# A decoder layer with 32 experts on one core: half of w_down taken with the expert groups, and half of the gate summed over eight chunks in PSUM

## The chip, the cores and the metric

The kernel runs on one core of a Trainium2 chip. The metric is the device time of one execution in microseconds (us); a profiled execution shows in addition its span, from the first to the last instruction of the trace. All positions ("at 372.0 us") are counted from the span's start.

## The reference, cut to what matters

One layer on 256 tokens of width 2048, all in fp32: attention, then a mixture of 32 experts (top 2 of one group of 8), then a gate, then a norm.

```
m   = rms_norm(h)
hid = silu(m @ w_gate[e]) * (m @ w_up[e]) * combine[:, e]     # 32 experts, 2048 -> 256
h   = h + sum over e of hid[e] @ w_down[e]                    # 256 -> 2048
n   = rms_norm(h)
h   = h + sigmoid(n @ w_ple_gate) * (p @ w_ple)              # 2048 -> 2048, 256 -> 2048
out = rms_norm(h)
```

The weights of this part have to be read once: w_gate and w_up 64 MiB each, w_down 64 MiB, w_ple_gate 16 MiB, w_ple 2 MiB.

## The kernel before

**Groups of experts.** The experts are taken four at a time, in 8 groups g = 0 to 7. Each expert holds at most 32 tokens, so a group's rows fill the 128 partitions. `gather` (in group 0 `first_rows` with its `part` and `turn`, one 512-column block each) picks the tokens with 0/1 matmuls and writes them, transposed, to `xg`. `hidden` multiplies them by the weights: 16 loads of 1 MiB per group, taken in quarters (k, i) of four loads, k for w_gate or w_up and i for the first or second half of the 2048 rows. The result, transposed, stays in `hid_all` to the end. Then `load_down`, `places` (the place mask `pw`, which holds the token's weight where the token stands), `down` (the product `dn`, copied to `y`) and `spread_rows` (y put back to its tokens, in plain fp32, and added to `acc[0]`) do block 0 of w_down, which is columns 0 to 511.

**The tail.** The other 1536 columns of w_down come after the last group, in `BLOCKS` 1 to 4 (512, 512, 256 and 256 columns), because the gate's input n needs a block of h that is complete. A pass over a block has units `u`: one group each in blocks 1 and 2 (8 units), two groups each in blocks 3 and 4 (4 units). A unit loads 2 MiB of w_down (`load_rows`), makes the product (`down_rows`, which splits the weighted result into a high part `y_hi` and a low part `y_lo` in the fast format fp32r) and adds it to the tokens' rows (`add_rows`, with 0/1 masks `held`, made by `weigh` during block 1). Between the two it takes some pieces of the gate of the block that was finished before (`PACE` says how many). One piece is 128 rows by 512 columns of w_ple_gate, cut into `wh` on ScalarE and `wl` on VectorE (`split_w`, two pieces ahead) and used in six matmuls (L974 to L976). `operand` transposes a finished block into `n_hi` and `n_lo`. Each block's gate is summed in PSUM over its own 4 (or 2) chunks of 128 rows and then copied or added to `z` by ScalarE or VectorE (L1040, L1042). The last unit of block 4, the last two chunks of the gate and the final norm follow (`last_rows_in`, `last_operand`, `finish`, `norm_rows`).

**The ring.** All weights go through 22 slots of 1 MiB (`Ring`). A load takes the slot that was used longest ago and waits until its last reader is done; `keep=True` holds a slot for good. SP issues all these loads in the order in which the code asks for them. `acc[1]` to `acc[3]` take two slots before group 7, `extra` and `emb` take three before group 2, `n_hi`, `n_lo` and `y` take five at the tail's start.

**The branch.** Before group 7 a branch (L901, `tc.If`) leads to `overflow`, for experts with more than 32 tokens; it isn't taken on these inputs. Every engine passes it; SP has half of group 7's 16 loads of w_gate and w_up ahead of it and half behind it.

Of the kernel before, what the change touches and what calls it, by code (L numbers as in the profile page):

```python
# [44 lines left out]
ON_V = (0, 1, 2, 3, 4)  # L45
CUT_G = (0, 5, 6)
# [39 lines left out]
def layer(ctx, tc, T, out):  # L86
# [628 lines left out]
    def load_experts(g, k):  # L715


        ws = []
        name, v = (("wg", w_gate), ("wu", w_up))[k]
        for i in range(2):  # L720
            parts = []
            for q in range(4):
                e = 4 * g + q
                if (g, k, i, q) == (0, 1, 1, 3):
                    w = hid_all.rearrange("p g c r -> p (g c r)").rearrange("p (c f) -> p c f", f=DE)
                else:
                    w = ring.tile([P, NC // 2, DE], name)
                if g:
                    nc.sync.dma_start(w, v[e].rearrange("(p c) f -> p c f", c=NC)[:, 8 * i : 8 * i + 8, :])
                else:  # L730
                    nc.sync.dma_start(
                        w.rearrange("p (b c) f -> p b c f", b=2),
                        v[e].rearrange("(b p c) f -> p b c f", b=4, c=4)[:, 2 * i : 2 * i + 2],
                    )
                parts.append(w)
            ws.append(parts)
        return ws

    def hidden(g, xg, ws, before=lambda k, i, c: None):

        gu = pse.tile([P, 2, DE], F32, name="gu", tag="gu")
        for k in range(2):
            for i in range(2):
                for c in range(8):
                    before(k, i, c)
                    for q in range(4):
                        PE.matmul(  # L747
                            gu[32 * q : 32 * q + 32, k, :], xg[:, 8 * i + c, 32 * q : 32 * q + 32], ws[2 * k + i][q][:, c, :],
                            start=(i == 0 and k == 0 and c == 0), stop=(i == 1 and c == 7), skip_group_check=True,
                        )  # L750
# [12 lines left out]
    def place_weights(g, gw):  # L763

        for t in range(NT):
# [3 lines left out]
        return gw  # L769

    def places(g, pw):
        gw = place_weights(g, exs.tile([P, NT, P], F32, name="gw", tag="gw"))
# [3 lines left out]
        A.copy(pw, tp[:, 0:S])  # L776

    def products(dn, g, wd):
        for c in range(2):
            for q in range(4):  # L780
                PE.matmul(  # L781
                    dn[32 * q : 32 * q + 32, :], hid_all[:, g, c, 32 * q : 32 * q + 32], wd[c][:, q, :],
                    start=(c == 0), stop=(c == 1),
                )

    def down(g, wd, y):

        dn = psk.tile([P, 512], F32, name="dn", tag="dn")
        products(dn, g, wd)
        A.copy(y, dn)  # L790

    def spread_rows(g, b, y, pw):
# [48 lines left out]
    def embedding():  # L841

        pin = extra[:, 0 : D - 512].rearrange("p (t d) -> p t d", t=NT)[:, :, 0:PLE]
# [3 lines left out]
        wple, slots = [], []  # L847
# [24 lines left out]

    xg = exq.tile([P, NC, P], F32, name="xg", tag="xg")
    with tc.manual_schedule(engines={mybir.EngineType.PE, mybir.EngineType.DVE, mybir.EngineType.Activation}):
        ws = load_experts(0, 0) + load_experts(0, 1)
# [5 lines left out]
        part(2)  # L881

        def rest_of_rows(k, i, c):
            if (k, i, c) == (0, 0, 4):
                turn(2)
                part(3)
            elif (k, i, c) == (0, 1, 0):
                turn(3)

        hidden(0, xg, ws, rest_of_rows)  # L890

    for g in range(n_groups):
        if g:
            ws = load_experts(g, 0)
        if g == n_groups - 1:
            rest = [ring.tile([P, 2, NT, 512], "acc", keep=True) for _ in range(2)]
            acc += [rest[b // 2][:, b % 2] for b in range(3)]
            for b in range(1, 4):
# [4 lines left out]
        if g == 2:  # L903
            extra = ring.tile([P, D], "late", keep=True)
# [3 lines left out]
        if g:  # L908
            ws += load_experts(g, 1)
            xg = exq.tile([P, NC, P], F32, name="xg", tag="xg")  # L910
            gather(g, xg)
            hidden(g, xg, ws, lambda k, i, c: next(blocks) if g in (2, 3) and c == 7 else None)
        wd = load_down(g, 0)
        if g == 0:
            weights()
        pw = exs.tile([P, S], F32, name="pw", tag="pw")
        places(g, pw)
        y = exs.tile([P, 512], F32, name="y", tag="y")
        down(g, wd, y)
        spread_rows(g, 0, y, pw)  # L920
# [42 lines left out]
    def load_gate(b, part):  # L963

        base, n = BLOCKS[b]
        chunks = n // P
        width = D // chunks
        rows = T["w_ple_gate"][0][base : base + n].rearrange("(q c) n -> q c n", c=chunks)
        return ring.load(rows[:, :, part * width : (part + 1) * width], [P, chunks, width], "wpg", True), ring.last
# [11 lines left out]
    def cuts():  # L981

        for b in range(len(BLOCKS) - 1):
            chunks = BLOCKS[b][1] // P
            for part in range(chunks):
                w, slot = load_gate(b, part if b < len(BLOCKS) - 2 else 1 - part)
                for n in range(4):
                    i, k = n // chunks, n % chunks
                    whl = split_w(w[:, k, 512 * i : 512 * i + 512], 512)
                    if n == 3:  # L990
                        ring.free([slot])
                    yield whl
# [27 lines left out]
    def gate(pieces):  # L1020

        for b in range(len(BLOCKS) - 1):
            chunks = BLOCKS[b][1] // P
            for cb in range(4) if b < len(BLOCKS) - 2 else (2, 3, 0, 1):
                ps = psf.tile([P, 1024], F32, name="ps", tag="mm")
                for k in range(chunks):
                    whl = pieces.next()
                    for t in range(NT):
                        gate_part(ps[:, t * 512 : (t + 1) * 512], t, CHUNK[b] + k, whl, k == 0, k == chunks - 1)
                    if k == chunks - 1:  # L1030
                        zb = z[:, :, cols(cb)]
                        pv = ps.rearrange("p (t n) -> p t n", t=NT)
                        if b:
                            if b == len(BLOCKS) - 2 and cb < 2:

                                held_ps[cb] = pv
                                zb = (pv, zb)
                            else:
                                zb = (zb, zb)
                            V.tensor_tensor(zb[0], pv, zb[1], ALU.add)  # L1040
                        else:
                            A.copy(zb, pv)  # L1042
                    yield
# [7 lines left out]
    def finish(t, cb, ps):  # L1051
        i = 4 * t + cb
        sg = extra[:, 512 * (i % 4) : 512 * (i % 4) + 512]
# [52 lines left out]

    wrow = brt[:, NC : NC + n_groups]
# [3 lines left out]
    held = [v[1][:, 4 + g, :] for v in (n_hi, n_lo) for g in range(4)]  # L1111

    pw_all = {g: extra[:, 256 * i : 256 * i + 256] for i, g in enumerate((0, 1, 4, 5))}
    y_all = extra[:, 1024:1536]

    def whole(gs, b):
        return b == len(BLOCKS) - 1 and gs[0] in pw_all

    y = ring.tile([P, 2, 512], "y", F32R, True)
    y_hi, y_lo = y[:, 0, :], y[:, 1, :]  # L1120

    def weigh(g):
        gw = place_weights(g, extra[:, 1536:1792].rearrange("p (t q) -> p t q", t=NT))
        yield
        tp = psk.tile([P, 512], F32, name="tpw", tag="sc", bufs=2)
        for t in range(NT):
            PE.transpose(tp[:, t * P : (t + 1) * P], gw[:, t, :], ident)
        V.tensor_reduce(wrow[:, g : g + 1], tp[:, 0:S], AX.X, ALU.add)  # L1128
        V.tensor_scalar(held[g], tp[:, 0:S], 0.0, None, ALU.is_gt)
        if g in pw_all:  # L1130
            A.copy(pw_all[g], tp[:, 0:S])
        yield
# [142 lines left out]
```

## Time and profile before

| | before |
|---|---|
| median of 3 runs | 906.3 us (905.25 to 906.84) |
| the profiled execution: its own time | 907.42 us |
| its span | 905.7 us |
| TensorE matmul busy | 828.0 us (91%) |
| VectorE, ScalarE busy | 407.6 us (45%), 303.2 us (33%) |
| moved by DMA | 279.54 MB, mean 309 GB/s |

The span has four stretches: attention and its projections to about 356 us, group 0 to 7 from there to about 702 us, the passes over the blocks of w_down with the gate from there to about 871 us, and a last stretch without loads. "Busy" counts a matmul from its start to its end; matmuls overlap, so a stretch in which TensorE is busy all the time may still hold room.

### The profile page before, as it was taken

How to read it: one execution, taken by the hardware profiler on the slowest of the kernel's cores; microseconds unless marked ns; L12 is line 12 of the kernel's file. 1: busy time of each engine (PE TensorE's matmuls, PEld its weight loads, DVE VectorE, ACT ScalarE, POOL GpSimd, SP SyncE). 2: the span in 40 equal slices, each digit the busy share in tenths (PEclk: the TensorE clock that was granted, in tenths of full speed). 3: DMA queues.
4: the chain of work that ended last, by engine and by line, in shares of the span. 5: the costliest groups of instructions: out<-in, count | busy, mean ns of one | idle time of the engine just before them, and what ended most of it. 6: DMA issues, size and time to landing. Idle time of an engine off the chain costs nothing. (4 is left out here: it accounts for less than half of the span.)

```text
span 905.7 us, 15013 instructions
## 1 busy us (share of the span) xinstructions
PE 828.0 (91%) x6074; PEld 613.3 (68%) x6074; DVE 407.6 (45%) x878; ACT 303.2 (33%) x633; POOL 74.7 (8%) x93
## 2 busy tenths in 40 slices
PE   9999999999999999999999988886596799989993
PEld 8998987899788886577756655553272445557762
DVE  4788667655555554221011202020110776656657
ACT  5657555644554453000021000000000534334354
POOL 3055233300000001000000000000100000000022
PEclk9999999999999999999999999988898999999997
DMA  9972434445699476599999999999899999999962
GB/s 302 369 227 94 162 118 140 140 142 185 221 391 356 148 283 226 209 410 419 415 412 419 412 418 414 417 413 418 312 414 396 386 386 386 387 367 356 362 219 93
DMA packets 105500, 279.54 MB, mean 309 GB/s; under 512 B 9488, under 2 KB 28240, under 8 KB 90704
## 3 DMA queue, kind: packets, MB, share of 16 engines
q1 hardware_dynamic: 104576, 278.45, 81.9%
q8 instruction: 50, 0.82, 0.4%
q0 software_dynamic: 320, 0.05, 0.2%
q14 instruction: 26, 0.21, 0.1%
q10 hardware_dynamic: 528, 0.01, 0.0%
HBM read 276.39 MB, written 2.10 MB: 307 GB/s over the span
## 5 line engine op out<-in xcount | busy, mean ns | idle before, releaser
L261 DVE TENSOR_TENSOR wl<-w,wh 128x512 fp32r<-128x512 f32 (+1 forms) x208 | 140.3, 681 | 108.3 <-ACT wh L260 104.6
L260 ACT ACTIVATE wh<-w 128x512 fp32r<-128x512 f32 (+1 forms) x208 | 127.0, 615 | 122.0 <-PE ps L280 56.1
L279 PE MATMUL ps<-xn_hi,wh 128*128 128x256 f32 x416 | 118.5, 285 | 0.0
L281 PE MATMUL ps<-xn_hi,wl 128*128 128x256 f32 x416 | 117.9, 283 | 0.2 <-DVE wl L261 0.2
L686 PEld LDWEIGHTS px<-gr,h 128*128 128x128 f32 x448 | 100.9, 310 | 25.3 <-issue 13.1
L280 PE MATMUL ps<-xn_lo,wh 128*128 128x256 f32 x416 | 117.7, 283 | 0.0
L686 PE MATMUL px<-gr,h 128*128 128x128 f32 x448 | 104.6, 386 | 10.4 <-DVE gr L676 7.2
L747 PE MATMUL gu<-wu,xg 128*32 128x256 f32 x1008 | 77.7, 421 | 26.6 <-DMA wu<-in_w_up_dram 26.6
L687 DVE TENSOR_TENSOR xg<-px,gmoe 128x512 f32<-128x512 f32 x28 | 19.3, 690 | 147.2 <-PE gu L747 100.7
L747 PEld LDWEIGHTS gu<-wu,xg 128*32 128x32 f32 x1008 | 37.6, 121 | 63.8 <-DMA wu<-in_w_up_dram 36.0
L279 PEld LDWEIGHTS ps<-xn_hi,wh 128*128 128x128 f32 x416 | 78.5, 189 | 1.6 <-issue 1.5
L281 PEld LDWEIGHTS ps<-xn_hi,wl 128*128 128x128 f32 x416 | 78.4, 188 | 1.6 <-issue 0.9
L280 PEld LDWEIGHTS ps<-xn_lo,wh 128*128 128x128 f32 x416 | 78.4, 189 | 0.4 <-issue 0.3
L752 ACT ACTIVATE hs<-gu 128x256 f32<-128x256 f32 x8 | 3.1, 384 | 219.6 <-PE gu L747 219.6
L747 PE MATMUL gu<-wg,xg 128*32 128x256 f32 x1024 | 65.2, 387 | 3.4 <-DMA wg<-in_w_gate_dram 3.4
L781 PE MATMUL dn<-wd,hid_all 128*32 128x512 f32 (+1 forms) x640 | 62.7, 513 | 3.7 <-DMA wd<-in_w_down_dram 3.6
L747 PEld LDWEIGHTS gu<-wg,xg 128*32 128x32 f32 x1024 | 33.6, 111 | 30.3 <-DMA wg<-in_w_gate_dram 4.4
L514 PE MATMUL ps<-wh,mixed 128*128 128x512 f32 x128 | 51.1, 399 | 0.0
L513 PE MATMUL ps<-wl,mixed 128*128 128x512 f32 x128 | 51.1, 399 | 0.0
L512 PE MATMUL ps<-wh,mixed 128*128 128x512 f32 x128 | 51.0, 398 | 0.0
L974 PE MATMUL ps<-wh,n_hi 128*128 128x512 f32 x112 | 46.5, 416 | 1.4 <-ACT wh L260 1.4
L975 PE MATMUL ps<-wl,n_hi 128*128 128x512 f32 x112 | 44.4, 396 | 0.8 <-DVE wl L261 0.8
(287 smaller groups left out, 1183.3 us busy)
## 6 DMA issues: line engine op xcount, KB each, us to landing
wg<-in_w_gate_dram SPq DMA_DIRECT2D x64, 1024.0 KB, 16.9
wd<-in_w_down_dram SPq DMA_DIRECT2D x64, 1024.0 KB, 14.4
wu<-in_w_up_dram SPq DMA_DIRECT2D x63, 1024.0 KB, 19.9
w<-in_w_in_dram SPq DMA_DIRECT2D x32, 1024.0 KB, 5.7
w<-in_w_out_dram SPq DMA_DIRECT2D x16, 1024.0 KB, 5.4
wpg<-in_w_ple_gate_dram SPq DMA_DIRECT2D x16, 1024.0 KB, 14.1
h<-in_x_dram SPq DMA_DIRECT2D x8, 256.0 KB, 10.0
w<-in_w_in_dram SPq DMA_DIRECT2D x4, 512.0 KB, 11.0
```

The lines of the kernel that those rows point to most:

```text
L260: A.activation(wh[:, :n], wv, AF.Copy)
L261: V.tensor_tensor(wl[:, :n], wv, wh[:, :n].bitcast(F32), ALU.subtract)
L279: PE.matmul(o, fh, xn_hi[:, c, :], start=(c == 0 and f % 2 == 0), stop=False, skip_group_check=True)
L280: PE.matmul(o, fh, xn_lo[:, c, :], start=False, stop=False, skip_group_check=True)
L281: PE.matmul(o, fl, xn_hi[:, c, :], start=False, stop=(c == NC - 1), skip_group_check=True)
L512: PE.matmul(o, mh, wh, start=(kc == 8), stop=False, skip_group_check=True)
L513: PE.matmul(o, mh, wl, start=False, stop=False, skip_group_check=True)
L514: PE.matmul(o, ml, wh, start=False, stop=(kc == 7), skip_group_check=True)
L686: PE.matmul(px[:, k, :], h_v[:, t, c + k, :], gr[:, t, :], start=(k == 0 and t == 0), stop=(t == 1), skip_group_check=True)
L747: PE.matmul(gu[32 * q : 32 * q + 32, k, :], xg[:, 8 * i + c, 32 * q : 32 * q + 32], ws[2 * k + i][q][:, c, :], start=(i == 0 and k == 0 an ...
L781: PE.matmul(dn[32 * q : 32 * q + 32, :], hid_all[:, g, c, 32 * q : 32 * q + 32], wd[c][:, q, :], start=(c == 0), stop=(c == 1),)
L974: PE.matmul(o, nh, whl[0], start=start, stop=False, skip_group_check=True)
```

## The change

More of w_down is taken with the groups, and the tail has one pass fewer.

- `load_down` fetches columns 0 to 1023 in four loads (two experts, 1024 columns each), so rows of 4 KB in place of rows of 2 KB. `down` runs for blocks 0 and 1 in each group (`EARLY = 2`), in the high and low parts that the tail uses.
- `places` makes the 0/1 mask `held` and the weight `wrow` in each group; `weigh` is gone.
- The tail begins with block 2. The gate of blocks 0 and 1 together is summed over eight chunks in PSUM, one half (1024 columns) at a time (`PLAN`), and written once; all gate loads are rows of 4 KB. A unit of block 2 takes four pieces in place of two (`PACE`).
- One slot each for `acc[1]` and `acc[2]` together, `held` and `yy` is kept from group 0 on; `extra` is given back after group 3.
- In group 0 the quarters come in the order (w_gate, first half), (w_up, first half), (w_gate, second half), (w_up, second half), with the rest of `part` and `turn` between the second and the third.
- All 16 loads of w_gate and w_up of group 7 stand ahead of the branch, its w_down behind it.
- The last unit of block 4, and two others that used one plain fp32 matmul per mask (`whole`), use the high and low parts as the rest do.

```diff
+EARLY = 2
+PLAN = (((0, 1), (0, 1)), ((2,), (0, 1)), ((3,), (1, 0)))
-PACE = ((0,) + (2,) * 7, (0,) + (2,) * 7, (2, 4, 4, 4), (4, 3, 1, 0))
+PACE = ((2,) + (4,) * 7, (2, 4, 4, 4), (4, 3, 1, 0))
...
-    def load_down(g, b):
+    def load_down(g):
         v = w_down[4 * g : 4 * g + 4].rearrange("e (p c) d -> c p e d", c=2)
-        return [ring.load(v[c, :, :, 512 * b : 512 * b + 512], [P, 4, 512], "wd") for c in range(2)]
+        ws = [[ring.load(v[c, :, 2 * i : 2 * i + 2, 0:1024], [P, 2, 1024], "wd") for i in range(2)] for c in range(2)]
+        return [[ws[c][q // 2][:, q % 2, :] for q in range(4)] for c in range(2)]
...
-        A.copy(pw, tp[:, 0:S])
+        V.tensor_reduce(wrow[:, g : g + 1], tp[:, 0:S], AX.X, ALU.add)
+        V.tensor_scalar(held[:, g, :], tp[:, 0:S], 0.0, None, ALU.is_gt)
...
+    def weighted(g, dn, y):
+        w = wrow[:, g : g + 1]
+        A.activation(y[:, 0], dn, AF.Copy, scale=w)
+        V.scalar_tensor_tensor(y[:, 1], dn, w, y[:, 0].bitcast(F32), ALU.mult, ALU.subtract)
+
+    def down(g, b, wd):
+        dn = psk.tile([P, 512], F32, name="dn", tag=("dn", "tp")[b])
+        products(dn, g, wd, slice(512 * b, 512 * b + 512))
+        y = yy[:, b]
+        weighted(g, dn, y)
         for t in range(NT):
             sc = psk.tile([P, 512], F32, name="sc", tag="sc", bufs=2)
-            PE.matmul(sc, pw[:, t * P : (t + 1) * P], y, start=True, stop=True)
+            for j in range(2):
+                PE.matmul(sc, held[:, g, t * P : (t + 1) * P], y[:, j], start=(j == 0), stop=(j == 1))
             a = acc[b][:, t, :]
-            V.tensor_tensor(a, h[:, t, 0:512] if g == 0 and b == 0 else a, sc, ALU.add)
+            V.tensor_tensor(a, h[:, t, 512 * b : 512 * b + 512] if g == 0 else a, sc, ALU.add)
...
-        ws = load_experts(0, 0) + load_experts(0, 1)
+        ws = load_experts(0, ((0, 0), (1, 0), (0, 1), (1, 1)))
+        wd = load_down(0)
...
+        if g in (0, n_groups - 1):
+            rest = ring.tile([P, 2, NT, 512], "acc", keep=True)
+            acc += [rest[:, b] for b in range(2 if g == 0 else 1)]
         if g:
-            ws = load_experts(g, 0)
+            ws = load_experts(g, order)
+        else:
+            held = ring.tile([P, n_groups, S], "held", F32R, True)
+            yy = ring.tile([P, 2, 2, 512], "y", F32R, True)
...
-    def load_gate(b, part):
+    def load_gate(b, k, half):
-        return ring.load(rows[:, :, part * width : (part + 1) * width], [P, chunks, width], "wpg", True), ring.last
+        return ring.load(rows[:, k : k + 2, 1024 * half : 1024 * half + 1024], [P, 2, 1024], "wpg", True), ring.last
...
-        for b in range(1, len(BLOCKS)):
-            op = operand(b - 1)
+        for b in range(EARLY, len(BLOCKS)):
+            ops = [operand(i) for i in (range(EARLY) if b == EARLY else (b - 1,))]
```

The change moves instructions at three places. First SP's queue where the loads of group 0 end (wg, wu and wd are the loads of w_gate, w_up and w_down; the one load into `hid_all` is the last of group 0's w_up, which borrows that tile). Before:

```order
L731 DMA wg<-in_w_gate_dram 128x2x1024 x8
L731 DMA wu<-in_w_up_dram 128x2x1024 x7
L77 DMA wd<-in_w_down_dram 128x4x512 x2
L729 DMA wg<-in_w_gate_dram 128x2048 x5
L731 DMA hid_all<-in_w_up_dram 128x2x1024
L900 TENSOR_LOAD cnt_i
```

and now:

```order
L735 DMA wg<-in_w_gate_dram 128x2x1024 x4
L735 DMA wu<-in_w_up_dram 128x2x1024 x4
L735 DMA wg<-in_w_gate_dram 128x2x1024 x4
L735 DMA wu<-in_w_up_dram 128x2x1024 x3
L83 DMA wd<-in_w_down_dram 128x2x1024 x4
L735 DMA hid_all<-in_w_up_dram 128x2x1024
L919 TENSOR_LOAD cnt_i
```

The five loads of group 1 that stood ahead of `hid_all` stand behind it now, and two more of w_down are in their place: 23 loads before, 20 now.

Second TensorE in group 0, where its rows are picked (L698 or L704, `part`), transposed (L709 or L715, `turn`) and multiplied (L747 or L751; a quarter is 32 matmuls). Before:

```order
L709 MATMUL px_4018<-ident,acc_3913 128x128 x4
L698 MATMUL px_4024<-h,gr 128x512 x2
L747 MATMUL gu<-wg,xg 32x256 x16
L709 MATMUL px_4045<-ident,acc_3913 128x128 x4
L698 MATMUL px_4051<-h,gr 128x512 x2
L747 MATMUL gu<-wg,xg 32x256 x16
```

and now:

```order
L715 MATMUL px_4026<-ident,acc_3913 128x128 x4
L751 MATMUL gu<-wg,xg 32x256 x32
L751 MATMUL gu<-wu,xg 32x256 x32
L704 MATMUL px_4097<-h,gr 128x512 x2
L704 MATMUL px_4101<-h,gr 128x512 x2
```

The first quarter, whose end gives four slots back, is no longer cut in two and has one `part` fewer ahead of it.

Third SP's queue from group 6 over the branch into the tail (the instructions of the branch that isn't taken are left out; wpg are loads of the gate's weights). Before:

```order
L729 DMA wg<-in_w_gate_dram 128x2048 x8
L729 DMA wu<-in_w_up_dram 128x2048 x8
L77 DMA wd<-in_w_down_dram 128x4x512 x2
L729 DMA wg<-in_w_gate_dram 128x2048 x4
L901 COMPARE_AND_BRANCH
...
L901 UNCONDITIONAL_BRANCH
L729 DMA wg<-in_w_gate_dram 128x2048 x4
L729 DMA wu<-in_w_up_dram 128x2048 x8
L77 DMA wd<-in_w_down_dram 128x4x512 x6
L77 DMA wpg<-in_w_ple_gate_dram 128x4x512
```

and now:

```order
L83 DMA wd<-in_w_down_dram 128x2x1024 x4
L733 DMA wg<-in_w_gate_dram 128x2048 x8
L733 DMA wu<-in_w_up_dram 128x2048 x8
L920 COMPARE_AND_BRANCH
...
L920 UNCONDITIONAL_BRANCH
L83 DMA wd<-in_w_down_dram 128x2x1024 x4
L83 DMA wd<-in_w_down_dram 128x4x512 x2
L83 DMA wpg<-in_w_ple_gate_dram 128x2x1024
```

Behind the branch stood twelve loads of w_gate and w_up; now group 7's w_down stands there at once.

## Rows read from the trace of the kernel before

**Rows 1.** The page, DMA in 40 slices of the span: GB/s moved

```profile
GB/s 302 369 227 94 162 118 140 140 142 185 221 391 356 148 283 226 209 410 419 415 412 419 412 418 414 417 413 418 312 414 396 386 386 386 387 367 356 362 219 93
```

**Rows 2.** Windows: stretch, length, busy PE, PEld, DVE, ACT, POOL, clock, DMA, GB/s

```profile
375.00:625.00 250.00, 227.94 (x2128) 153.86 (x2120) 37.17 (x90) 15.48 (x33) 0.00 (x0) 0.97 1.02 415
690.00:800.00 110.00, 99.23 (x580) 54.17 (x581) 68.53 (x130) 42.10 (x75) 0.00 (x0) 0.99 1.04 386
800.00:870.00 70.00, 67.15 (x484) 47.78 (x482) 43.56 (x66) 27.64 (x56) 1.27 (x1) 1.00 1.07 361
```

**Rows 3.** TensorE in group 0: start, length, line, operation [idle before it]

```profile
363.98 1.88 PE L698 MATMUL px<-h,gr 128*128 128x512 f32 x4
...
365.79 1.93 PE L747 MATMUL gu<-wg,xg 128*32 128x256 f32 x32
...
368.24 1.88 PE L698 MATMUL px<-h,gr 128*128 128x512 f32 x4
...
370.05 1.93 PE L747 MATMUL gu<-wg,xg 128*32 128x256 f32 x32
```

**Rows 4.** Timeline of SP: the first load behind a full ring

```profile
372.00 1.29 SPq L729 DMA_DIRECT2D wg<-in_w_gate_dram  x3
```

**Rows 5.** Windows at the ring's restart and at the branch, columns as above

```profile
365.00:370.00 5.00, 5.00 (x43) 2.13 (x41) 0.69 (x1) 1.88 (x2) 0.00 (x0) 1.00 0.00 0
652.00:653.00 1.00, 0.00 (x0) 0.00 (x0) 0.00 (x0) 0.00 (x0) 0.00 (x0) 1.00 0.15 57
653.00:654.00 1.00, 0.00 (x0) 0.00 (x0) 0.00 (x0) 0.00 (x0) 0.00 (x0) 1.00 0.02 8
655.00:659.00 4.00, 3.85 (x18) 3.85 (x18) 1.10 (x6) 0.00 (x0) 0.00 (x0) 0.57 0.87 297
```

**Rows 6.** The branch's line on SP: duration ns, first and last start

```profile
L901 SPq EVENT_SEMAPHORE  x8: 17/17/17, 651.4 to 654.3; - x8
L901 SPq COMPARE_BRANCH  x1: 50/50/50, 636.8 to 636.8; - x1
```

**Rows 7.** SP's four loads behind the branch: first and last start; issue to landing

```profile
L729 SPq DMA_DIRECT2D wg<-in_w_gate_dram x4: 338/376/1852, 654.5 to 657.3; - x4
DMA to landing us min/median/max: 5.3/9.5/12.6
```

**Rows 8.** TensorE and its weight loads (PEld) in the tail

```profile
697.32 1.92 PE L781 MATMUL dn<-wd,hid_all 128*32 128x512 f32 x16
...
704.12 1.23 PE L947 MATMUL tpn<-ident,acc 128*128 128x128 f32 x8
...
707.59 0.70 PE L1186 MATMUL sc<-y,n_hi 128*128 128x512 f32 x2 [2.02 <-DVE n_lo L953]
...
770.83 1.92 PE L781 MATMUL dn<-wd,hid_all 128*32 128x512 f32 x16
...
776.58 1.92 PE L781 MATMUL dn<-wd,hid_all 128*32 128x512 f32 x16
...
808.50 0.16 PEld L781 LDWEIGHTS dn<-wd,hid_all 128*32 128x32 f32 x8 [0.35 <-issue]
...
809.62 1.02 PEld L781 LDWEIGHTS dn<-wd,hid_all 128*32 128x32 f32 x24 [0.96 <-DMA wd<-in_w_down_dram]
...
818.72 1.93 PE L781 MATMUL dn<-wd,hid_all 128*32 128x256 f32 x32
...
827.29 1.93 PE L781 MATMUL dn<-wd,hid_all 128*32 128x256 f32 x32
...
836.40 0.64 PE L781 MATMUL dn<-wd,hid_all 128*32 128x256 f32 x8
```

**Rows 9.** Timeline of TensorE where block 4 ends and behind it

```profile
868.30 1.89 PE L1186 MATMUL sc<-late 128*128 128x256 f32 x8
...
870.12 0.50 PE L1100 MATMUL ps<-n_hi 1*128 1x512 f32 x1
...
871.53 1.50 PE L781 MATMUL dn<-wd,hid_all 128*32 128x256 f32 x24 [0.34 <-DMA wd<-in_w_down_dram]
```

More of the change, by code (lines that the diff above doesn't have):

```diff
@@ L713, in first_rows, with load_half @@
         return part, turn
-    def load_experts(g, k):
-        ws = []
+    def load_half(g, k, i):
+        parts = []
         name, v = (("wg", w_gate), ("wu", w_up))[k]
[L720 to L733, printed above, removed]
-                    )
-                parts.append(w)
-            ws.append(parts)
-        return ws
@@ L739, in hidden @@
[L739 to L750, printed above, removed]
+        for q in range(4):
+            e = 4 * g + q
+            if (g, k, i, q) == (0, 1, 1, 3):
+                w = hid_all.rearrange("p g c r -> p (g c r)").rearrange("p (c f) -> p c f", f=DE)
+            else:
+                w = ring.tile([P, NC // 2, DE], name)
+            if g:
+                nc.sync.dma_start(w, v[e].rearrange("(p c) f -> p c f", c=NC)[:, 8 * i : 8 * i + 8, :])
+            else:
+                nc.sync.dma_start(
+                    w.rearrange("p (b c) f -> p b c f", b=2),
+                    v[e].rearrange("(b p c) f -> p b c f", b=4, c=4)[:, 2 * i : 2 * i + 2],
+                )
+            parts.append(w)
@@ new lines, in load_half, with load_experts, hidden @@
+        return parts
+    def load_experts(g, order):
+        return {(k, i): load_half(g, k, i) for k, i in order}
+    def hidden(g, xg, ws, between=lambda k, i: None):
+        gu = pse.tile([P, 2, DE], F32, name="gu", tag="gu")
+        for n, (k, i) in enumerate(ws):
+            for c in range(8):
+                for q in range(4):
+                    PE.matmul(
+                        gu[32 * q : 32 * q + 32, k, :], xg[:, 8 * i + c, 32 * q : 32 * q + 32], ws[k, i][q][:, c, :],
+                        start=(n == 0 and c == 0), stop=(n == 3 and c == 7), skip_group_check=True,
+                    )
+            between(k, i)
@@ L841, in embedding @@
     def embedding():
+        extra = ring.tile([P, D], "late", keep=True)
+        slots = [ring.last]
         pin = extra[:, 0 : D - 512].rearrange("p (t d) -> p t d", t=NT)[:, :, 0:PLE]
@@ L902, in layer @@
                 overflow()
-        if g == 2:
-            extra = ring.tile([P, D], "late", keep=True)
+        if g == EMB[0]:
             emb = [ring.tile([P, NT, 1024], "emb", keep=True) for _ in range(2)]
@@ L908, in layer @@
         if g:
-            ws += load_experts(g, 1)
             xg = exq.tile([P, NC, P], F32, name="xg", tag="xg")
             gather(g, xg)
-            hidden(g, xg, ws, lambda k, i, c: next(blocks) if g in (2, 3) and c == 7 else None)
-        wd = load_down(g, 0)
-        if g == 0:
+            hidden(g, xg, ws, lambda k, i: next(blocks) if g in EMB else None)
+            wd = load_down(g)
+        else:
             weights()
[L916 to L920, printed above, removed]
+        places(g)
+        for b in range(EARLY):
+            down(g, b, wd)
     pool_pe.__exit__(None, None, None)
@@ L981, in cuts @@
     def cuts():
[L983 to L992, printed above, removed]
+        for bs, halves in PLAN:
+            for half in halves:
+                for b, k, _, _ in pairs(bs):
+                    w, slot = load_gate(b, k, half)
+                    for n in range(4):
+                        whl = split_w(w[:, n % 2, 512 * (n // 2) : 512 * (n // 2) + 512], 512)
+                        if n == 3:
+                            ring.free([slot])
+                        yield whl
     def last_cuts(ws):
@@ L1110, in layer @@
     held_ps = {}
[L1111 to L1132, printed above, removed]
     def load_rows(gs, b):
@@ L1196, in layer @@
         steps = gate(pieces)
-        for b in range(1, len(BLOCKS)):
-            op = operand(b - 1)
-            if b < 3:
-                units = [(g,) for g in range(n_groups)]
-            else:
-                units = UNITS[b - 3]
+        turn = 0
+        for b in range(EARLY, len(BLOCKS)):
+            ops = [operand(i) for i in (range(EARLY) if b == EARLY else (b - 1,))]
+            units = [(g,) for g in range(n_groups)] if b < 3 else UNITS[b - 3]
             for u, gs in enumerate(units):
```

182 lines of the change are left out of this document (78 added, 104 removed).

## The prediction

> **What bounds the kernel now.** I read the page's 40 slices first [rows 1]. From about 372 us the DMA moves 380 to 420 GB/s nearly to the end, with two holes: the 17th slice (209) and the 29th (312). The windows say what sets these rates [rows 2]: in the expert groups, where 16 of 18 loads have rows of 8 KB, 415 GB/s at a DMA share of 1.02; in the passes over blocks 1 and 2, rows of 2 KB, 386 at 1.04; in blocks 3 and 4, mostly rows of 1 KB, 361 at 1.07. The queue is full in all three, and TensorE waits for it. It is busy 228 of 250 us in the groups, 99 of 110 and 67 of 70 in the tail, so in blocks 3 and 4 it has next to no room.
>
> The holes are two places where SP may not issue. At 365 to 370 nothing moves [rows 5]: the ring is full, and the first slots come free when the first quarter of group 0 is multiplied. That quarter has 64 matmuls in two pieces of 32, with a `part` ahead of each [rows 3]; it ends at 371.9, and the next load is issued at 372.0 [rows 4]. I count the queue from 373.0. The second hole is the branch: SP reaches it at 636.8 and passes eight semaphores at 651.4 to 654.3 [rows 6], one for each chain of loads in flight. Behind 636.8 it issues nothing, so the queue runs dry (57 and 8 GB/s at 652 to 654, [rows 5]); I take the drain at 652.5. The four loads behind the branch are issued from 654.5 to 657.3, and the last lands 12.6 later [rows 7], at 669.9: 17.4 us from the drain until four loads are there, where a full queue needs 10. Before the change that costs TensorE little beyond a gather that it does meanwhile, because these four belong to the second half of w_gate, which it needs later.
>
> **The prices.** A load is 1.0486 MB. 2 KB rows: 1.0486 / 0.386 = 2.72 us. A group of 18 loads at 415 GB/s takes 45.48; less two of 2.72, the 16 with 8 KB cost 2.50 each. Three loads of the last window (two of 1 KB, one of the gate) take 8.71; less about 2.65 for the gate's, a 1 KB one costs 3.03. No row shows 4 KB alone: it lies between 2.50 and 2.72. I take a time per row that is a constant and a part by length, through 2 KB and 8 KB; in it 4 KB costs 2.575, nearer to the 8 KB end. This choice weighs, since 28 such loads stand ahead of the point that decides below.
>
> The two rows that are 2.50 and 2.72 differ by 8.5%. The Trainium skill (DMA: Bandwidth & Descriptors, Why small descriptors are slow) states a fixed cost of about 3 cycles for a packet, beside 32 bytes moved in a cycle; by it 2 KB would cost 3.5% more than 8 KB, less than half of what the rows show, and 4 KB only 2.3% less than 2 KB, an estimate of 2.66. With that price the sum below would be 2.3 us later.
>
> **The change, step by step.**
>
> *Start.* 20 loads stand ahead of the full ring in place of 23, and one slot each goes to `acc`, `held` and `yy`. The first quarter runs where the `part` of 363.98 stood, undivided: about 2 × 1.9 us, to 367.7. So the restart comes 4.2 us earlier and I count the queue from 368.8.
>
> *To the second hole.* Before: 97 loads of 8 KB rows (two are w_ple) and 12 of 2 KB from the restart to the drain; 97 × 2.50 + 12 × 2.72 + 0.7 (a quarter load for `extra`) = 276.1 us against 279.5 measured (373.0 to 652.5), a factor of 1.012. After: five loads of group 1 move behind the restart and twelve of group 7 ahead of the branch, which makes 114 of 8 KB; w_down of groups 1 to 6 is 24 of 4 KB in place of 12 of 2 KB: (114 × 2.503 + 24 × 2.575 + 0.7) × 1.012 = 352.0. The queue drains at 368.8 + 352.0 = 720.8.
>
> *Behind it.* Now the four loads behind the branch are group 7's w_down, which TensorE needs at once. All of group 7's w_gate and w_up have landed by the drain and are multiplied a few us later; then it sits idle until 720.8 + 17.4 + 0.3 (4 KB rows) = **738.5**. The old order had twelve loads between the branch and the first thing that waits for w_down. This is the step on which I rest the forecast: the hole, which was mostly hidden, is now in TensorE's path.
>
> *TensorE from 738.5.* (1) The rest of group 7: half of block 0's products 0.95, block 1's 1.9 (16 matmuls of 512 columns, [rows 8]), eight adds 2.1: 5.0. (2) Block 2. A unit with two pieces of the gate takes 776.58 − 770.83 = 5.75, one with four 827.29 − 818.72 = 8.57 [rows 8], so a piece is 1.41 and four adds are 5.75 − 1.86 − 2.82 = 1.07. Seven units of four pieces 60.0, the first with two 5.75, 16 transposes 2.4 (8 take 1.23), the start's wait for `n_lo` 2.0: 70.1. (3) Blocks 3 and 4 as now, 808.50 to 870.12 = 61.6, less the waits for w_down (0.96 at 809.62, 0.38 at 836.40) and 0.8, since the plain fp32 adds at 868.30 take 1.82 and the split ones about 1.0: 59.5. (4) From 870.12 to the end 35.6, less the wait 0.34 at 871.53 [rows 9], less 0.9 for the last fp32 adds, plus 0.4 for the low part: 34.8. (5) The clock. After an idle stretch as short as that of the branch now, the granted clock was 0.57 over 655 to 659 [rows 5], between the levels 1.2 and 2.4 GHz: 4 × 0.43 = 1.7. The sum is 171.1.
>
> 738.5 + 171.1 = 909.6, against a span of 905.7: +3.9. The profiled execution's own time is 907.42, so 911.3 for a profiled one; that execution is 1.1 above the median, and against the median I get 906.3 + 3.9 = **910.2**.
>
> *Hidden.* In each group TensorE has block 1's 16 products to do as well, 1.9 us, and its adds, which cost in all about what the plain fp32 ones of one block do now. Its busy time of 228 / 250 × 45.5 = 41.5 becomes 43.4, in a period of (16 × 2.503 + 4 × 2.575) × 1.012 = 51.0, so the DMA covers it (without cover 8 × 1.9 = 15 us). VectorE's fewer adds of the gate's sums (eight chunks in PSUM) shorten work that is 69 of 110 us busy in the tail [rows 2], off the path: nothing. `held` made in the groups lies on VectorE, 37 of 250 busy: nothing. The ring has three slots fewer, 17 to 19 for loads, where SP's eight chains [rows 6] hold eight in flight: nothing, as long as TensorE follows the queue.
>
> **The rivals.**
>
> *B, the queue sets the end (faster).* If TensorE kept up, only the queue would count. All loads after the restart: before 109 × 2.503 + 58 × 2.717 + 16 × 3.03 + 4 × 2.575 = 489.2, after 114 × 2.503 + 44 × 2.575 + 16 × 2.717 + 16 × 3.03 = 490.6, so +1.4, less the 4.2 of the earlier restart: −2.8, 903.5. The hole costs the same in both. For it: the tail is at a DMA share over 1.0 now. Against it: from the hole on TensorE would need at most 902.9 − 738.5 = 164.4 us, 6.7 under the sum. It decides if the four loads land some 5 us sooner or the stage of block 2 is shorter than its rows.
>
> *C, the units of block 2 go at the slower pace.* One four-piece unit took 827.29 to 836.40 = 9.11 in place of 8.57, waiting for the split of the weights. Seven like this: +3.8, 914.0. For it: block 2 wants 4 pieces in 8.57 us, 0.47 a us, where block 2 of now has 2 in 5.75, 0.35. Against it: VectorE loses the gate's adds.
>
> *D, 4 KB rows cost nearly what 2 KB rows do.* With 2.72, 28 × 0.142 × 1.012 = +4.0 to 738.5, 914.2. With 2.50 it is −2.0, 908.2, inside A.
>
> **How the numbers follow.** A (TensorE in the tail behind the late w_down) 0.48, with its own range 906 to 914; B 0.28, 901.5 to 906; C 0.12; D 0.12. About 0.2%, 1.8 us, is what a measurement here tells from no change: 904.5 to 908.1. Below it: 0.8 of B and 0.04 of A, 0.25. Inside: 0.2 of B and 0.24 of A, 0.17. Above: the rest of A, C and D, 0.58. The range 903 to 914.5 leaves out the lower part of B (0.11) and the upper of C and D (0.09).
>
> **What would show it.** The restart near 368 and not 372; the drain at the branch near 721 (some 4 us later if D holds); TensorE idle for over 10 us there, until group 7's w_down lands near 738, with a low clock behind it; in block 2 no waits for w_down, units of 8.6 us (9.1 if C holds); the queue below a share of 1.0 in the tail, where now it is above. If TensorE still waits for w_down in block 2 to 4, B is right and I am wrong; so I am if it does not idle at the branch, or if the groups' rate with the 4 KB rows is lower than now by over 3%.

## The result, and the profile of the changed kernel

| | before | changed |
|---|---|---|
| median (4 runs each) | 906.57 us (905.25 to 907.26) | 914.07 us (912.74 to 915.59) |
| ratio to before | | 1.0085, 95% interval 1.0062 to 1.0108 |
| the profiled execution: own time, span | 907.42, 905.7 us | 915.59, 913.9 us |

The changed kernel is slower by 7.5 us, where the sum had 3.9 (910.2 against 906.3). 914.07 lies inside the range of 903.0 to 914.5, near its upper end. The differences of single executions below go by the spans, which are 8.2 us apart.

The page's line of GB/s in 40 slices, now (a slice is 22.8 us), is the one that answers to [rows 1]:

```profile
GB/s 303 369 219 95 180 98 137 138 171 188 228 393 312 183 277 47 350 417 373 418 413 420 409 420 416 416 419 413 420 415 417 324 397 394 394 363 373 362 60 93
```

The first hole lies earlier, and is not smaller: 47 and 350 in the 16th and 17th slice, where it was 226 and 209. The second has moved from the 29th slice to the 32nd (324), and a small one is new, in the 19th (373). The next rows are windows: stretch, length, busy time of the engines, granted clock, DMA share, GB/s.

```profile
365.00:370.00 5.00, 5.00 (x97) 2.99 (x92) 0.00 (x0) 0.00 (x0) 0.00 (x0) 1.00 0.24 54
415.00:420.00 5.00, 5.00 (x100) 3.00 (x94) 0.00 (x0) 0.00 (x0) 0.00 (x0) 1.00 0.63 212
540.00:640.00 100.00, 85.06 (x726) 52.84 (x722) 18.70 (x42) 4.26 (x8) 0.00 (x0) 0.93 1.01 417
722.00:724.00 2.00, 0.47 (x11) 0.30 (x15) 0.00 (x0) 0.00 (x0) 0.00 (x0) 1.00 0.06 25
724.00:735.00 11.00, 6.88 (x70) 2.58 (x62) 1.18 (x3) 2.24 (x4) 0.00 (x0) 1.00 0.92 347
736.00:742.00 6.00, 4.41 (x16) 0.97 (x16) 0.75 (x1) 0.69 (x1) 0.00 (x0) 0.50 1.05 393
743.00:752.00 9.00, 6.67 (x43) 3.01 (x42) 5.73 (x10) 2.96 (x7) 0.00 (x0) 1.00 1.04 396
754.00:760.00 6.00, 5.66 (x13) 4.15 (x14) 2.97 (x6) 1.70 (x4) 0.00 (x0) 0.52 1.04 395
762.00:820.00 58.00, 58.00 (x300) 38.74 (x292) 31.84 (x48) 27.09 (x46) 0.00 (x0) 1.00 1.05 384
800.00:860.00 60.00, 60.00 (x414) 43.65 (x413) 35.69 (x57) 27.17 (x52) 0.00 (x0) 1.00 1.07 366
```

The groups run at 417 GB/s, where they had 415. The small hole is the stretch of 415 to 420 (212 GB/s): the ring has no free slot, and SP waits 16.9 us for TensorE's first quarter of group 1, so about 2 us of loading are lost. The queue is dry at 722 to 724, one to two us behind the forecast drain. From 762 to 860 TensorE is busy in every us, 58.00 of 58 and 60.00 of 60, where before it was 99 of 110 and 67 of 70 [rows 2]. The DMA share is still above 1.0 there: its engines hold transfers all the time, but TensorE no longer waits for them. So the share alone does not tell which of the two sets the end; the busy time and the missing waits do.

SP's timeline at the restart, and the branch's line, as in [rows 4] and [rows 6]:

```profile
367.64 6.27 SPq L733 DMA_DIRECT2D wg<-in_w_gate_dram  x6
```

```profile
L920 SPq EVENT_SEMAPHORE  x8: 17/17/17, 715.9 to 723.8; - x8
```

The last load ahead of the branch lands at 723.5 (issued at 703.5, 20.0 to landing). The four loads behind the branch, as in [rows 7]:

```profile
L83 SPq DMA_DIRECT2D wd<-in_w_down_dram x4: 389/405/849, 723.9 to 725.4; - x4
DMA to landing us min/median/max: 5.2/8.3/11.4
```

So the fourth lands at 736.8, 13.3 us behind the last one ahead of the branch. In the kernel before these two points lie at 653.9 (636.4 + 17.5) and 669.9 [rows 7], 16.0 us apart. A full queue needs 10 for four loads, so the hole costs the queue 6.0 us there and 3.3 here.

And the timeline of TensorE from the branch to the end, to be read with [rows 8, 9]: start, length, line, operation, and in brackets the idle time before it with what ended it.

```profile
723.52 3.64 PE L751 MATMUL gu<-wu,xg 128*32 128x256 f32 x58 [1.87 <-SPq L920]
...
731.70 1.05 PE L786 MATMUL dn<-wd,hid_all 128*32 128x512 f32 x4 [1.21 <-DMA wd<-in_w_down_dram]
734.26 1.05 PE L786 MATMUL dn<-wd,hid_all 128*32 128x512 f32 x4 [1.51 <-DMA wd<-in_w_down_dram]
736.83 2.00 PE L786 MATMUL dn<-wd,hid_all 128*32 128x512 f32 x6 [1.51 <-DMA wd<-in_w_down_dram]
...
751.19 1.20 PE L962 MATMUL tpn<-ident,acc 128*128 128x128 f32 x8 [1.45 <-DVE n_lo L968]
754.08 0.79 PE L992 MATMUL ps<-wh,n_hi 128*128 128x512 f32 x1 [1.70 <-ACT wh L266]
...
760.88 1.92 PE L786 MATMUL dn<-wd,hid_all 128*32 128x512 f32 x16
...
820.12 1.93 PE L786 MATMUL dn<-wd,hid_all 128*32 128x256 f32 x32
...
879.29 0.49 PE L1119 MATMUL ps<-n_hi 1*128 1x512 f32 x1
```

The wait of 1.87 at 723.52 has the name of the branch; the last load of w_up lands just then, at 723.5. After the wait that ends at 736.83, no wait for a load follows. That is the point from which TensorE's work alone sets the end. Set against the sum of the prediction:

| stretch | forecast | measured |
|---|---|---|
| the last load of group 7's w_down is there | 738.5 | 736.8 |
| from there to block 2's second unit (760.88): the terms 5.0, 5.75, 2.4, 2.0 and the clock's 1.7 | 16.9 | 24.05 |
| seven units of block 2, to 820.12 | 60.0 | 59.2 |
| blocks 3 and 4, to 879.29 | 59.5 | 59.2 |
| the end, to 913.9 | 34.8 | 34.6 |
| from the last load to the end | 171.1 | 177.1 |

Four terms are within 2 us. One is off by 7: the stretch from group 7's last products to the second unit. The granted clock stands at 0.50 (the level of 1.2 GHz) over 736 to 742 and at 0.52 over 754 to 760: in these windows that is 6 × 0.50 + 6 × 0.48 = 5.9 us if all of it counts, and 4.41 × 0.50 + 5.66 × 0.48 = 4.9 if only TensorE's busy time does, where 1.7 were priced. TensorE's waits in this stretch are 0.76, 0.88, 1.45, 1.70 and 0.25, in all 5.0 us, where the prediction had 2.0. About 1 us is left; the low clock at the windows' edges (0.68 at 742 to 743, 0.65 at 759 to 760) can be most of it.

The same point can be read in the kernel before, where the last load of group 7's first w_down block is issued at 674.9:

```profile
L77 SPq DMA_DIRECT2D wd<-in_w_down_dram x1: 1505/1505/1505, 674.9 to 674.9; - x1
DMA to landing us min/median/max: 20.4/20.4/20.4
```

It lands at 695.3, 210.4 us ahead of the end. So this w_down is there 736.8 − 695.3 = 41.5 us later now, and the stretch behind it, waits included, is 210.4 − 177.1 = 33.3 us shorter. The difference, 8.2 us, is that of the two spans.

### The profile page after: what moved, and what is told of

Read it like the earlier page. It is cut to its first block, busy times and chain, and to the rows that moved or that the text cites. A ratio compares the mean times of both kernels' runs of the same rounds, so it can differ in the third digit from the quotient of the medians.

```text
span 913.9 us, 14912 instructions
## 1 busy us (share of the span) xinstructions
PE 839.7 (92%) x6058; PEld 616.6 (67%) x6058; DVE 403.5 (44%) x853; ACT 300.2 (33%) x622; POOL 73.2 (8%) x92
## 5 line engine op out<-in xcount | busy, mean ns | idle before, releaser
L692 PE MATMUL px<-gr,h 128*128 128x128 f32 x448 | 107.3, 389 | 11.9 <-DVE gr L682 7.8
L751 PE MATMUL gu<-wu,xg 128*32 128x256 f32 x1008 | 79.8, 433 | 23.5 <-DMA wu<-in_w_up_dram 21.5
L786 PE MATMUL dn<-wd,hid_all 128*32 128x512 f32 (+1 forms) x640 | 78.7, 530 | 4.2 <-DMA wd<-in_w_down_dram 4.2
L751 PEld LDWEIGHTS gu<-wu,xg 128*32 128x32 f32 x1008 | 39.0, 124 | 62.0 <-DMA wu<-in_w_up_dram 28.5
L794 ACT ACTIVATE y<-dn,brt 128x512 fp32r<-128x512 f32 (+1 forms) x40 | 23.8, 601 | 131.3 <-PE dn L786 119.1
L751 PE MATMUL gu<-wg,xg 128*32 128x256 f32 x1024 | 64.9, 381 | 1.3 <-DMA wg<-in_w_gate_dram 1.3
L751 PEld LDWEIGHTS gu<-wg,xg 128*32 128x32 f32 x1024 | 33.9, 110 | 26.9 <-issue 3.2
## 6 DMA issues: line engine op xcount, KB each, us to landing
wd<-in_w_down_dram SPq DMA_DIRECT2D x64, 1024.0 KB, 14.9
w<-in_w_in_dram SPq DMA_DIRECT2D x4, 512.0 KB, 11.1
```

What stands on the lines that cost most here:

```text
L692: PE.matmul(px[:, k, :], h_v[:, t, c + k, :], gr[:, t, :], start=(k == 0 and t == 0), stop=(t == 1), skip_group_check=True)
L751: PE.matmul(gu[32 * q : 32 * q + 32, k, :], xg[:, 8 * i + c, 32 * q : 32 * q + 32], ws[k, i][q][:, c, :], start=(n == 0 and c == 0), stop= ...
L786: PE.matmul(dn[32 * q : 32 * q + 32, :], hid_all[:, g, c, 32 * q : 32 * q + 32], wd[c][q][:, cs], start=(c == 0), stop=(c == 1),)
```

## The experiments

Each ratio below is taken to the kernel before, which ran on the same chip beside them (medians 906.48, 905.58 and 905.64 us in the three jobs). The changed kernel itself did not run in those jobs; at its ratio of 1.0085 it would stand at 914.2, 913.3 and 913.3, uncertain by 2 us, and differences to it are meant so.

**The branch where it was.** Is the hole the cause?

```diff
-            ws = load_experts(g, order)
+            ws = load_experts(g, order[:2] if g == n_groups - 1 else order)
...
             with tc.If(worst > CAP):
                 overflow()
+            ws |= load_experts(g, order[2:])
```

> The changed kernel with half of group 7's loads behind the branch again: four of w_gate ahead of it, twelve behind it and then its w_down. Theory H (the hole at the branch was hidden before and now lies in TensorE's path, as the prediction had it): TensorE has work ahead of w_down again, the time falls by 5 to 10 us, to 904 to 909. Theory T (the hole costs the queue the same wherever it stands; w_down of group 7 lands as late as now, and from there TensorE's own work sets the end): 912 to 915, with the last load of that w_down landing within 1.5 us of 737.

Measured: 912.68 us, ratio 1.0068 (1.0051 to 1.0085), 1.5 us below the changed kernel. The queue now runs dry 30 us earlier (41 GB/s at 692 to 694), no wait for w_down is left in group 7, and the time is nearly the same. Its timeline:

```profile
727.26 5.71 PE L751 MATMUL gu<-wu,xg 128*32 128x256 f32 x58 [1.44 <-DMA wu<-in_w_up_dram]
...
735.24 4.18 PE L786 MATMUL dn<-wd,hid_all 128*32 128x512 f32 x32
...
757.64 1.92 PE L786 MATMUL dn<-wd,hid_all 128*32 128x512 f32 x16
```

Here TensorE waits for the last w_up instead, and the products go on without a break at 735.24. The last load of w_down lands at 737.5 (issued at 717.2, 20.3 to landing), as theory T has it; it is no longer waited for. The tail's start waits just as long (1.45 and 1.70), and the second unit starts 3.2 us earlier. Twelve loads stand between the branch and w_down again, and they gave 1.5 us where theory H needed 5 to 10: theory H falls.

**The kernels without the branch.** What does the hole cost in either?

```diff
-            worst = nc.values_load(cnt_i[0:1, 0:1], min_val=0, max_val=S)
-            with tc.If(worst > CAP):
-                overflow()
```

> The kernel before without that branch (the same path is left out). Theory T: the queue sets the end here and the hole is 7.4 us of it: 6 to 8 us less, 898.5 to 900.5, so the distance between the two kernels stays 6 to 8 us without the hole. Had the hole been hidden before, as the prediction says: under 2 us less, 905 to 906.5.

Measured: 900.69 us, ratio 0.9951 (0.9934 to 0.9967), 4.9 us less. The hole was not hidden before. It is short of the 6 to 8 us of theory T and close to the 6.0 us that the hole costs the queue. (The profiled span is 8.1 us shorter, 897.6, but that execution is the shortest of its five.)

> The changed kernel without the branch before group 7 (the path for experts with more than 32 tokens is left out). Theory T: group 7's w_down lands 7.4 us earlier (the hole of 17.4 us less the 10 that four loads take), near 729.5, TensorE's work from there is the same and its clock falls less: 7 to 9 us less, 905 to 907. If the hole costs the changed kernel more than the kernel before: a larger gain here than there.

Measured: 910.48 us, ratio 1.0051 (1.0034 to 1.0069), 2.8 us less than the changed kernel; the span is 5.4 us shorter. That misses the expected 7 to 9, and the trace says why. The four loads of group 7's w_down:

```profile
L83 SPq DMA_DIRECT2D wd<-in_w_down_dram x4: 367/378/1462, 706.8 to 714.3; - x4
DMA to landing us min/median/max: 20.0/20.1/20.2
```

The last lands at 734.5, 2.3 us earlier than in the changed kernel and not 7.4 (3.4 if both are counted from the ring's restart, which comes 1.1 later here). That fits the 3.3 us that the hole costs the queue there: the 17.4 of the kernel before did not carry over. TensorE waits for none of the four in this trace; group 7's products start at 731.86, behind the last w_up. What the pair shows besides is the comparison: without the hole the two kernels are 9.8 us apart, with it 7.5. It does not explain that the changed kernel is slower.

**Filler matmuls against the low clock.**

```diff
+FILL = 2
...
+                if fill and q % 2 == 0 and c + q:
+                    busy(held[:, 0, 0:32].bitcast(F32), FILL)
...
+                        if b == EARLY:
+                            idle = psf.tile([P, 1024], F32, name="idle", tag="mm")
+                            for _ in range((10, 12)[n]):
+                                PE.matmul(idle[:, 0:S], held[:, 0, 0:P], held[:, 0, :], start=True, stop=True)
```

> The changed kernel with filler matmuls where TensorE waits: two after each of the first three loads of group 7's w_down, ten and twelve behind the two lots of transposes at the tail's start; group 7's products are written out ahead of its adds. Theory T with the low clock as the part that the prediction mis-sized: the granted clock is 1.0 from 735 to 760, and the time falls by 4 to 7 us, to 907 to 910. If the waits there and not the clock cost the time: a fall of under 2 us, 912 to 914. Theory H says nothing of it beyond 1.7 us, its own price of the clock.

Measured: 910.62 us, ratio 1.0049 (1.0032 to 1.0066), 3.6 us less than the changed kernel, just under the expected 4 to 7. Filler matmuls are matmuls whose result nothing reads. The windows show what it does:

```profile
736.00:742.00 6.00, 6.00 (x31) 1.81 (x31) 2.69 (x4) 1.38 (x2) 0.00 (x0) 1.00 1.05 392
743.00:752.00 9.00, 8.23 (x52) 5.46 (x51) 5.79 (x12) 5.11 (x12) 0.00 (x0) 1.00 1.03 392
754.00:760.00 6.00, 6.00 (x35) 3.54 (x34) 3.31 (x5) 2.12 (x4) 0.00 (x0) 1.00 1.03 395
```

The granted clock is 1.00 in all three. From the last load of w_down to the second unit it takes 755.95 − 736.40 = 19.55 us in place of 24.05:

```profile
736.40 2.77 PE L789 MATMUL dn<-wd,hid_all 128*32 128x512 f32 x20
...
755.95 1.50 PE L789 MATMUL dn<-wd,hid_all 128*32 128x512 f32 x12
```

So 4.5 us came back with the clock. Without its 1.7 for the clock the forecast of this stretch is 15.2, so 4.4 us are left over it. The largest part are the tail's waits, which fillers only fill: from the first eight transposes to the second eight and from there to the gate's first matmul it takes 2.7 and 2.9 us in both traces. The order of group 7's products was written out with the fillers, and is not told apart from them.

**Less work for TensorE.** Is it the bound from there?

```diff
-        PE.matmul(o, nh, whl[1], start=False, stop=False, skip_group_check=True)
+        if n >= 8:
+            PE.matmul(o, nh, whl[1], start=False, stop=False, skip_group_check=True)
```

> The changed kernel without the products of the low part of the gate's weights for blocks 0 and 1: 64 of TensorE's matmuls at 0.233 us less, 14.9 us, with all loads, copies and splits as now. That part of the gate is left out of the output. Theory T: TensorE sets the end in the tail, so the time falls until the queue sets it, by 9 to 13 us, to 901 to 905, and TensorE waits for w_down in blocks 3 and 4 again. If the queue or the splitting sets the end already: under 3 us, 911 to 914.

Measured: 903.13 us (10 runs), ratio 0.9967 (0.9952 to 0.9983): 11.1 us less than the changed kernel for 14.9 us of matmuls, inside the expected 9 to 13. And the wait for w_down in block 3 is back, in the timeline of the weight loads:

```profile
808.61 1.02 PEld L786 LDWEIGHTS dn<-wd,hid_all 128*32 128x32 f32 x24 [1.22 <-DMA wd<-in_w_down_dram]
```

TensorE was the bound. The queue is close behind it now: 903.1 is near where rival B put the queue's end (903.5). That the queue sets the end here is not shown: the units of block 2 take 6.65 us and wait for no load, and this one wait is about 1 us.

**Less to load ahead of that point.**

```diff
-        ws = [[ring.load(v[c, :, 2 * i : 2 * i + 2, 0:1024], [P, 2, 1024], "wd") for i in range(2)] for c in range(2)]
-        return [[ws[c][q // 2][:, q % 2, :] for q in range(4)] for c in range(2)]
+        ws = [ring.load(v[c, :, :, 0:512], [P, 4, 512], "wd") for c in range(2)]
+        return [[ws[c][:, q, :] for q in range(4)] for c in range(2)]
...
-        products(dn, g, wd, slice(512 * b, 512 * b + 512))
+        products(dn, g, wd, slice(0, 512))
```

> The changed kernel with the second 512 columns of w_down left out of the groups' loads (block 1 is multiplied with the columns of block 0, so its part of the output is not the reference's); TensorE, VectorE and ScalarE do all that they do now, and the queue has two 2 KB loads per group in place of four of 4 KB. Theory T: group 7's w_down lands earlier by what these loads cost the queue: 12 loads fewer and the rest dearer in groups 1 to 6, 29.5; two fewer ahead of the full ring, 5.0; two fewer in group 7, about 5. TensorE's work from there is as long as now, so the time falls by about 39, to 872 to 878. If TensorE were the bound in the groups too, or the tail had room: under 30, above 883.

Measured: 885.88 us, ratio 0.9789 (0.9765 to 0.9812): 27.4 us less, not 39. The trace says why it stops there:

```profile
674.91 14.26 PE L692 MATMUL px<-gr,h 128*128 128x128 f32 x64 [6.81 <-DVE gr L682]
689.10 7.11 PE L751 MATMUL gu<-wg,xg 128*32 128x256 f32 x128
696.03 7.09 PE L751 MATMUL gu<-wu,xg 128*32 128x256 f32 x128
...
705.50 4.46 PE L786 MATMUL dn<-wd,hid_all 128*32 128x512 f32 x18
```

Behind its 6.81 us at the branch TensorE does group 7 in one go, with no wait for a load: TensorE is the bound there too, and w_down comes 31 us earlier instead of 39. The groups ahead are near the same limit:

```profile
375.00:625.00 250.00, 239.63 (x2111) 155.79 (x2113) 58.11 (x129) 19.20 (x34) 0.00 (x0) 0.98 0.98 399
```

TensorE is busy 240 of 250 us there, and only from 603 on it waits for loads again. And the end follows group 7's w_down: from 705.50, where its products start and run without a wait, to the end (884.4) it is 178.9 us, against 177.1 from the last load in the changed kernel.

**Rows of 2 KB.** Is the price of the loads right?

```diff
+        return [[ring.load(v[c, :, :, 512 * b : 512 * b + 512], [P, 4, 512], "wd") for c in range(2)] for b in range(2)]
...
-        products(dn, g, wd, slice(512 * b, 512 * b + 512))
+        products(dn, g, [[w[:, q, :] for q in range(4)] for w in wd[b]], slice(0, 512))
```

> The changed kernel with its w_down in the groups loaded as four loads of 512 columns, rows of 2 KB, in place of 4 KB. Theory T: what the queue loses to group 7's w_down goes to the end in full: 28 loads at 2.72 in place of about 2.54 are 5 us, 917 to 920. By the prediction's price of 2.575 it is 4.0 us, by the price of 2.66 that the Trainium skill's rule would give (DMA: Bandwidth & Descriptors, Why small descriptors are slow) 1.7 us. If TensorE waits for something else: no change.

Measured: 915.29 us, ratio 1.0104 (1.0083 to 1.0124), 2.0 us more, which alone would not tell the prices apart. The groups' rate does:

```profile
540.00:640.00 100.00, 79.60 (x708) 49.20 (x708) 16.53 (x37) 3.57 (x7) 0.00 (x0) 0.91 1.02 412
```

A group's 20 loads take 20 × 1.0486 / 0.412 = 50.90 us here and 50.29 at the changed kernel's 417. Less 16 of 2.503, a 2 KB load is 2.71 and a 4 KB one 2.56, with 0.06 or so for a GB/s of reading: the prediction's 2.575 holds. The landings agree: the last load of group 7's w_down is there at 741.0 in place of 736.8, 4.2 us later, where the price makes 4.0 for 28 loads. The end takes only 2.0 of it; a likely reason, not tested alone, is that block 0's two loads now come ahead of block 1's, at 735.6, and TensorE starts on them sooner. By an estimate from the Trainium skill (DMA: Bandwidth & Descriptors, Why small descriptors are slow) the two prices would differ by 2.3%; the rates make it 5 to 6%, so the measurement decides against that figure here.

**The order of group 0, alone and undone.**

> The kernel before with the changed order in group 0 alone: its four quarters in the order of the change and the rest of part and turn between the second and the third. The ring's restart comes at 367.7 in place of 372.0. If the queue sets the end of the kernel before all the way from there: 4.2 us less, 902 to 903. If a part of it is taken back by a ring that stalls later, or TensorE's work in the tail holds some: 903 to 905. If TensorE sets the end: 905.5 to 907.

Its edit in the kernel before:

```diff
+        w4 = [load_experts(0, k, (i,)) for k, i in ((0, 0), (1, 0), (0, 1), (1, 1))]
+        ws = w4[0] + w4[2] + w4[1] + w4[3]
...
-        part(2)
...
-            if (k, i, c) == (0, 0, 4):
-                turn(2)
-                part(3)
-            elif (k, i, c) == (0, 1, 0):
-                turn(3)
+            if (k, i, c) == (0, 1, 0):
+                for b in range(2, 4):
+                    part(b)
+                for b in range(2, 4):
+                    turn(b)
```

Measured: 901.90 us (901.03 to 902.33), ratio 0.9950 (0.9933 to 0.9966), 4.6 us less than before. It beats both kernels, and gives the 4.2 us in full. The restart, from the timelines of TensorE and of SP:

```profile
360.59 3.70 PE L698 MATMUL px<-h,gr 128*128 128x512 f32 x8 [0.48 <-DVE gr L676]
369.42 1.28 SPq L729 DMA_DIRECT2D wg<-in_w_gate_dram  x3
```

In this execution the first rows are picked 1.7 us later than in the kernel before (358.91), so the restart comes at 369.4 and not at the expected 367.7; counted from the first rows it is 8.8 us, where it was 13.1 (358.91 to 372.00). The last load of group 7's first w_down block lands at 690.9 in place of 695.3, 4.4 us earlier, and the time follows it.

> The changed kernel with the order of group 0 as it was. The restart goes back from 367.7 to about 372. The changed kernel's ring stands again for about 2.4 us at 415 to 420 (212 GB/s in that window), for want of slots. If that stall stays: 4.2 us more, 917 to 918.5. If the early restart was only paid back there: 1.8 us more, 915 to 916.5.

That is the same edit undone in the changed kernel. Measured: 918.03 us (915.25 to 921.52), ratio 1.0130 (1.0102 to 1.0157), 4.7 us more. That agrees with 4.2 us there too, within the 2 us. But the stall at 415 to 420, for want of slots, is gone in this trace (408 GB/s), and a slower stretch shows at 440 to 540 (409 GB/s). In the kernel before with the early restart it is not there either (421 GB/s). So that stall takes both, the early restart and the fewer slots; what the three missing slots cost in all is not settled.

**The sums in PSUM.**

```diff
-PLAN = (((0, 1), (0, 1)), ((2,), (0, 1)), ((3,), (1, 0)))
+PLAN = (((0,), (0, 1)), ((1,), (0, 1)), ((2,), (0, 1)), ((3,), (1, 0)))
```

> The changed kernel with the gate summed in PSUM block by block again (blocks 0 and 1 apart, four chunks each, the second added to z by VectorE: four more adds of 1.2 us). The prediction has that part hidden: no change, 912 to 915. If VectorE's adds or the PSUM banks hold TensorE up in block 2: 2 to 5 us more, 915.5 to 918.5.

Measured: 916.84 us (912.78 to 918.73), ratio 1.0111 (1.0081 to 1.0140), 3.5 us more than the changed kernel by the medians. That is outside the 912 to 915 of "no change" and inside the range of the other theory, but the interval overlaps the changed kernel's, so the times alone do not decide. The trace speaks against the other theory's reason: the seven units of block 2 take 8.46 us as in the changed kernel.

```profile
762.56 1.92 PE L786 MATMUL dn<-wd,hid_all 128*32 128x512 f32 x16
...
821.77 1.93 PE L786 MATMUL dn<-wd,hid_all 128*32 128x256 f32 x32
```

The profiled execution is 3.1 us longer than the changed kernel's: 1.7 of it lie ahead of 762.56 and 1.4 behind 821.77, none between. Whether the eight chunks gain 0 to 3 us outside block 2 stays open.

## Why the prediction was right in its sign and short in its size

- **The start.** Right: the restart at 367.6 for 367.7, and the order worth 4.6 us in the kernel before and 4.7 in the changed one.
- **The drain and the price of 4 KB.** Right within 2 us and 0.02 us.
- **"The hole, which was mostly hidden, is now in TensorE's path."** This is the step that failed as a reason. The hole was not hidden before. By the end of group 7 TensorE had caught up with the queue and waited for the last load of w_up, so a later landing went on to the end:

```profile
689.95 5.09 PE L747 MATMUL gu<-wu,xg 128*32 128x256 f32 x58 [1.49 <-DMA wu<-in_w_up_dram]
```

Leaving the branch out there gave 4.9 us, of the 6.0 that the hole costs the queue. In the changed kernel the hole is smaller, 3.3 us, and gave 2.8 when it was left out and 1.5 when its place was given back. TensorE did not idle for over 10 us there: from 721.65 to 736.83 its waits are 1.87, 0.93, 0.46, 1.21, 1.51 and 1.51, in all 7.5, since it still had most of the last quarter of w_up to multiply. The date of 738.5 came out nearly right partly by luck: the drain was a us or two late, and the hole 2.7 us shorter than the one it was copied from.

- **What makes the change slower** is the count of loads that stand ahead of group 7's w_down. From the restart to its landing there are 114 of 8 KB rows and 28 of 4 KB in place of 109 and 14 of 2 KB: 46 us more by their prices. The earlier restart (4.4) and the shorter hole (2.7) come off, the stall for slots (about 2) comes on, and the landing is measured 41.5 us later. Only 33.3 us leave the stretch behind it. The sum had all these loads; it had the wrong reason for the loss.
- **TensorE sets the end from there.** Right, and shown from two sides: 11 us less for 14.9 us of matmuls, and the end moving with the start of group 7's products. Rival B would have needed 6.7 us less of TensorE's work than the sum had; there were 6 more. The sign that was named for it, a DMA share below 1.0 in the tail, did not come (1.05 and 1.07).
- **The clock's 1.7 us.** This is the mis-sized term. It was priced by the one low stretch of the kernel before; there were two, and fillers gave back 4.5 us along the path and 3.6 in the time. With 2.8 us more for the clock and waits of 5.0 in place of 2.0 it is nearly the whole difference between 171.1 and 177.1.
- **The range.** It held by little and not by its own reason. The prediction's own case, A, had 906 to 914, and 914.07 lies above it; the upper end of 914.5 was there for C and D, and neither came.
- **Units at the slower pace (rival C), 4 KB near 2 KB (rival D).** Neither came: the units take 8.46 us, and the 4 KB load 2.56.
- **Hidden work.** Block 1's products in the groups are covered at the period of 50 us, with little to spare: with fewer loads per group TensorE was busy 240 of 250 us and the queue fell to 399 GB/s. "Fewer slots: nothing" missed the stall at 415 to 420; what the slots cost in all is open.

## What to carry to other kernels

Moving work from a crowded tail into a stretch where an engine waits is free for that engine and not for the queue: count the loads that come ahead of the point from which the tail depends, and set their time against the work that the tail loses. A pause in the queue that no engine seems to wait for may still be paid at the end: look for the next wait for a load behind it, and leave the pause out once before calling it hidden. When a change has several parts, time each alone: here one of them, an order of a few matmuls that frees the first buffers sooner, was worth 4.6 us, and it was under a change that lost 7.5.

## What the runs showed of the hardware

The granted clock fell to 0.50 twice within 24 us. Ahead of the first fall TensorE was busy 6.88 of 11 us, in pieces of a us or two between loads; ahead of the second 6.67 of 9 us, with idle stretches of 1.45 and 1.70 us at its end. By windows of 1 us it was below 1.00 from 735 to 743 and from 752 to 760, at 0.50 in most of them. With fillers TensorE was busy 8.23 of 9 us ahead of the second and the clock stayed at 1.00. So the low clock cost about as much here as the waits of the tail's start: 4.5 us came back with the fillers, beside 5.0 us of waiting.

At the branch SP issued nothing until the loads in flight had landed: the last landing and the next issue were 653.9 and 654.5 in the kernel before, 723.5 and 723.9 in the changed one, and 693.1 and 693.3 with the branch where it was.
